# The retention blocks of a hybrid decoder layer: three products as f32 matmuls without splits, a mean of squares on ACT, a third raw weight buffer

## The chip, the cores and the metric

One core of one Trainium2 chip runs the whole kernel in one launch. The metric is the device time of an execution in microseconds (us), lower is better. The engines are TensorE (PE; its weight loads are shown as PEld), VectorE (DVE), ScalarE (ACT), GpSimd (POOL) and SyncE (SP), which only issues DMAs here.

## The reference

One inference step of a one-layer decoder, with a prompt of 1,024 positions and 8 samples of 4 positions, model width 1,024, all in f32. One input projection gives the columns of sliding-window attention, of retention (4 heads, key width 128, value width 256), of the retention gate and of two merge gates. The change is in the retention branch, which goes through the prompt in chunks of 128 positions:

```
scores = einsum('bihd,bjhd->bhij', q, k) * dmask
inner  = einsum('bhij,bjhe->bihe', scores, v)
cross  = einsum('bihd,bhde->bihe', q, s0) * q_decay
s_new  = exp(log_g * L) * s0 + einsum('bjhd,bjhe->bhde', k * k_decay, v)
o      = inner + cross
o      = o * rsqrt(mean(o * o, axis=-1) + EPS)      # per head, then silu(gate) * o
```

After it come two output projections, the merge through `w_o`, and a convolutional feed-forward of width 3 x 1,024.

## The kernel before, in words

**Products.** Most matmuls are done on split operands: a value x is written as hi = x rounded to fp32r (a copy on ACT) and lo = x - hi (on DVE or POOL; helper `split`, lines L228 and L223, on POOL L225), and `mm3` makes a product as hi·hi + hi·lo + lo·hi, three fp32r matmuls (L255, L256, L257). Operands that are plain f32 go to TensorE unsplit in a few places, the scores (L1113) and the sample attention (L731) among them.

**The stream.** The projections of the 16 pairs of column blocks (queries and keys, gates, merge gates) are a Python generator `stream`. Each pair has two halves j of the columns (528 of the 1,056 each), each half seven products of a Strassen-like scheme (A11, S1, A22, S2, A12, S4, S3), each product twelve matmuls of 264 columns into banks `ps_q`. ACT copies results out (L898); DVE adds others (L921 for S4, L923 for S3). `adv(n)` makes the generator go on by n products, so that other work can be traced between them.

**Weights of the stream.** `in_split(n)` loads the two raw weight tiles of a pair (`pair_weights`, L340 on the SP queue, 512 KB each) and makes seven split operands of them, one for each product (`w_split`: ACT L329, DVE L223). The buffer of every third raw tile comes from `wx["raw"]`, the others from the pool `wraw` of two; before the change `wx["raw"]` is `wraw` too, so there are two raw buffers in all. The operands of a pair are made while the second half of the pair before runs; its raw loads are traced at A22 in the first half of that pair.

**The sample blocks** come first between the products: `sample(h)` for 4 heads, each with 4 steps over pairs of samples. A step takes a state tile `s0` of 256 KB (loaded by `load_s0` on SP, L989; shown in the profile as `s`), splits it, makes its products with `kb` (L1033, L1035), updates it (L1036) and stores it from the POOL queue (L1038); three stream products stand between steps. `finish` is the per-head norm.

**The prompt blocks**: 32 blocks g, 8 for each head, are pipelined by hand. `front(g)` makes scores and the transpose of k (L1113, L1114) into one bank `ps_a` of two, masks the scores (L1116) and makes the split operands `sT`, `kt`, `vt`, `qs`; it is traced one block ahead, and `load_qk` (SP, L1084, three buffers) and `load_v` (POOL, L1091, four buffers) two blocks ahead of it. `middle(g)` makes inner and cross product into one bank and the state's product into another, updates `state` (L1144), splits it into `sts` for the next block, and calls `finish`. `tail(g)` of the block before turns the result by TensorE (L979) and multiplies it with the gate (L1163). Four stream products are traced with each block. In some blocks the tail also makes sums of `w_r` and `w_down` weights (`zt`) and stores.

**finish** squares with a sum along the row on ACT (L971), makes mean and epsilon on DVE (`rsqrt_mean`, L280), the power -0.5 on POOL (L282), and scales on ACT (L973).

**What sets the order.** The Tile framework turns the traced program into one instruction list for each engine: a scheduler places instructions by priority in traced order and by its own simulated times, and gives a pool's buffer to the next tile once all readers of the old one are placed. On the chip each engine and each DMA queue (SP's and POOL's) then works strictly through its list.

Of the kernel before, what the change touches and what calls it, by code (L numbers as in the profile page):

```python
# [9 lines left out]
F32 = mybir.dt.float32  # L10
# [3 lines left out]
ALU = mybir.AluOpType  # L14
# [106 lines left out]
def trunk(ctx, tc, I, O):  # L121
# [95 lines left out]
    def f32(ap):  # L217
        return ap.bitcast(F32)
# [546 lines left out]
    pa = ppool("pa", 2, ps_stack)  # L765
    pq = ppool("pq", 1, ps_stack)
    pb = ppool("pb", 2, ps_stack)
    wx["sum"], wx["raw"] = pool("wsum", 1, stack=sm_stack), wraw
    p2 = pool("p2", 1, stack=ph_stack)

    def quarters(t):
# [36 lines left out]
    def ST(name, shape, dt=F32, **kw):  # L808
        return rp.tile(list(shape), dt, name=name, **kw)
# [64 lines left out]
    def stream():  # L874

        early = (A11, S1, S2, A12, S4, S3)
        ws = in_split(ORDER[0])
        next(ws)
        ops = {p: next(ws) for p in early}
        last, nh = None, 0  # L880
        for i, n in enumerate(ORDER):
            for j in range(2):
                o = TT("pair")
                c11, c12, c21, c22 = (o[:, HW * q:HW * q + HW] for q in range(4))
                dst = {A12: c11, S1: c22, S2: c12, A22: c21}
                bk = [psum(pq, "q%d" % b)[:, :HW] for b in (0, 2)]
                b1 = pq.tile([P, 512], F32, name="ps_q1", tag="q1", bufs=2)[:, :HW]
                bk.insert(1, b1)
                if j:
                    nxt = {}  # L890

                def product(p, ps, t, j, dst):
                    for k in range(4):
                        xh, xl = xop(ex1, p, j, k)
                        mm3(ps, t[:, k], t[:, 4 + k], xh, xl, p in (A11, S1) and k == 0, k == 3,
                            skip_group_check=p not in (A11, S1))
                    if p in dst:
                        S.copy(out=dst[p], in_=ps)  # L898

                for p in (A11, S1, A22, S2, A12, S4, S3):  # L900
                    if p == A22:
                        if last is not None:
                            product(A22, *last)
                        if j == 0:
                            ops[A22] = next(ws)
                            if i + 1 < len(ORDER):
                                ws = in_split(ORDER[i + 1])
                                next(ws)
                        if last is not None:
                            yield  # L910
                        continue
                    if p == S2:
                        if nh < 2:
                            TE.matmul(bk[1], ops[p][:, 0], xop(ex1, p, j, 0)[0], start=True, stop=True)
                            S.copy(out=bk[1], in_=bk[0])
                        nh += 1
                    product(p, bk[{A11: 0, A12: 0, S2: 1, S3: 1, S1: 2, S4: 2}[p]], ops[p], j, dst)
                    if p == A11 and nh >= 2:
                        S.copy(out=bk[1], in_=bk[0])
                    if p == S4:  # L920
                        V.tensor_tensor(out=c12, in0=bk[2], in1=c12, op=add)  # L921
                    if p == S3:
                        V.tensor_tensor(out=c22, in0=bk[1], in1=c22, op=add)  # L923
                    if p == S2:
                        flush()
                    if j and i + 1 < len(ORDER):
                        nxt[p] = next(ws)
                    yield
                last = bk[1], ops[A22], j, dst
                PEND.append((pairs[n][2], j, o))  # L930
            if i + 1 < len(ORDER):
                ops = nxt
        product(A22, *last)
        flush()
        yield
# [31 lines left out]
    def finish(po, n, s, h, bufs=2):  # L967

        ssq = sml.tile([P, 1], F32, name="ss")[:n]
        o = ST("o", (P, 256), bufs=bufs)[:n]  # L970
        S.activation(o, po[:n, :256], AF.Square, accum_out=ssq)  # L971
        r = rsqrt_mean(ssq, 256, n, 1, oeps[:n, s, h:h + 1])
        S.mul(o, po[:n, :256], r)  # L973
        return o

# [8 lines left out]
    def load_s0(n):  # L984
        if n >= 2 * DB:
            return
        h, bb = n // 4, 2 * (n % 4)
        s0s_[n] = ST("s0", (P, 2, 256), bufs=4)
        ld.dma_start(out=s0s_[n], in_=I["state_ret"][0, bb:bb + 2, h].rearrange("b k e -> k b e"))  # L989

    def sample(h):
        gS = float(GAMMA[h] ** 4)
        dm = ST("dm", (P, P), bufs=2)
        ld.dma_start(out=dm, in_=I["dmask"][:, h, 1])
        qk8 = ST("qk8", (P, 2, NS), bufs=2)
        ld.dma_start(out=qk8, in_=qk_d[h].rearrange("i p t -> p i t")[:, :, :NS])
# [2 lines left out]
        r8 = ST("r8", (P, 2, P))  # L999
        for i in range(2):  # L1000
            S.copy(out=r8[:, i, :].rearrange("p (o t) -> p o t", o=4), in_=rep(qk8[:, i]))
        v8 = ST("v8", (P, 256), F32R, bufs=2)
        S.copy(out=v8[0:32], in_=vs)
        S.copy(out=v8[64:96], in_=vs)
        V.tensor_tensor(out=v8[32:64], in0=vs, in1=f32(v8)[0:32], op=sub)
# [14 lines left out]
        TE.matmul(po, h8[:, 0, 0:2 * NS], v8, start=True, stop=False)  # L1020
        for bb in range(0, DB, 2):
            s0 = s0s_[(h * DB + bb) // 2]
            load_s0((h * DB + bb) // 2 + 2)
            s0s = ST("s0s", (P, 2, 2, 256), F32R)
            split(s0s[:, 0], s0s[:, 1], s0)
            for b in range(2):
                q = q8[:, 2 * NS * (bb + b):2 * NS * (bb + b + 1)]
                for s in range(2):
                    TE.matmul(po, q, s0s[:, s, b], start=False, stop=bb + b == DB - 1 and s == 1)
            pk = ps_a()  # L1030
            for b in range(2):
                kb = ST("kb", (P, P), F32R, bufs=2)
                V.tensor_scalar(out=kb, in0=f32(h8)[:, 1], scalar1=bm[:, bb + b:bb + b + 1],  # L1033
                                scalar2=None, op0=mult)
                TE.matmul(pk[:, 256 * b:256 * b + 256], kb, v8, start=True, stop=True)  # L1035
            V.scalar_tensor_tensor(out=s0, in0=s0, scalar=gS,  # L1036
                                   in1=pk.rearrange("p (b e) -> p b e", b=2), op0=mult, op1=add)
            st.dma_start(out=O["ret_sample"][0, bb:bb + 2, h].rearrange("b k e -> k b e"), in_=s0)  # L1038
            yield
# [2 lines left out]
        V.tensor_tensor(out=os8, in0=po[0:NS], in1=os8, op=add)  # L1042
        S.copy(out=z8[:, h], in_=turn(pt, finish(os8, NS, 1, h, 1)))

    for n in range(2):
        load_s0(n)
    adv(18)
    for h in range(4):
        for _ in sample(h):
# [36 lines left out]
    def load_v(g):  # L1086
        if g >= NBLK:
            return
        h, tt = divmod(g, NB)
        vts[g] = ST("vt", (P, 2, 256), F32R, bufs=4)  # L1090
        st.dma_start(out=f32(vts[g][:, 1]), in_=v_d[h, tt])  # L1091

    def mask(h):
        dm = ST("dm", (P, P), bufs=2)
# [13 lines left out]
    def front(g, dm):  # L1108
        h, tt = divmod(g, NB)
        q, k = (qks[g][:, i] for i in range(2))  # L1110
        vt = vts[g]
        ps = ps_a()
        TE.matmul(ps[:, :P], k, q, start=True, stop=True)  # L1113
        TE.transpose(ps[:, P:2 * P], k, ident)  # L1114
        s32 = ST("s32", (P, P))
        V.tensor_tensor(out=s32, in0=ps[:, :P], in1=dm, op=mult)  # L1116
        sT = ST("sT", (P, 2, P), F32R, bufs=2)
        split(sT[:, 0], sT[:, 1], s32)
        kt = ST("kt", (P, 2, P), F32R, bufs=2)
        S.mul(kt[:, 0], ps[:, P:2 * P], kdec[:, 0, h:h + 1])  # L1120
        V.scalar_tensor_tensor(out=kt[:, 1], in0=ps[:, P:2 * P], scalar=kdec[:, 0, h:h + 1],
                               in1=f32(kt)[:, 0], op0=mult, op1=sub)
        split(vt[:, 0], vt[:, 1], f32(vt[:, 1]))
        qs = None
        if tt:
            qs = ST("qs", (P, 2, P), F32R, bufs=2)
            split(qs[:, 0], qs[:, 1], q, G)
        return ps, sT, kt, vt, qs

    def middle(g, ps, sT, kt, vt, qs):  # L1130
        h, tt = divmod(g, NB)
        gL = float(GAMMA[h] ** 128)
        vh, vl = vt[:, 0], vt[:, 1]
        pt = ps_b()
        po = pt[:, :256]
        mm3(po, sT[:, 0], sT[:, 1], vh, vl, True, tt == 0)
        if tt:
            sts = state["sts"]
            mm3(po, qs[:, 0], qs[:, 1], sts[:, 0], sts[:, 1], False, True)
        pk = ps[:, 256:]  # L1140
        mm3(pk, kt[:, 0], kt[:, 1], vh, vl, True, True)
        ns_ = ST("state", (P, 256), bufs=2)
        if tt:
            V.scalar_tensor_tensor(out=ns_, in0=state["s"], scalar=gL, in1=pk, op0=mult, op1=add)  # L1144
        else:
            V.tensor_copy(out=ns_, in_=pk)
        state["s"] = ns_
        if tt < NB - 1:
            sts = state["sts"] = ST("sts", (P, 2, 256), F32R)
            split(sts[:, 0], sts[:, 1], ns_)  # L1150
        else:
            st.dma_start(out=O["ret_prompt"][0, 0, h], in_=ns_)
        return pt, finish(po, P, 0, h)

# [566 lines left out]
```

## Time and profile before

| | |
|---|---|
| median of 3 runs | 1690.79 us (1689.51 to 1692.35) |
| the profiled execution's own time | 1689.79 us |
| its span, first to last instruction | 1688.0 us |
| mean granted TensorE clock | 0.992 |
| instructions | 32,984 |
| DMA | 273.92 MB, mean 162 GB/s |
| stream of the 16 pairs, by the starts of its matmuls | 273 to 729 us of the span |
| sample blocks, by the starts of their state products | 335 to 444 us |
| prompt blocks, by the starts of their scores and products | 456 to 698 us |

Busy times are shares of the span of one profiled execution. The records of matmuls are pipelined: a matmul of 264 columns is recorded with some 284 ns, and the next starts some 120 ns later, so prices of matmuls are taken from start to start. A wait on the weight load (PEld) and one on the matmul that follows it are the same stand of TensorE seen twice.

### The profile page before, as it was taken

What the parts mean: (1) busy time and instruction counts of PE and PEld (TensorE: products, weight loads), DVE (VectorE), ACT (ScalarE), POOL (GpSimd) and SP (SyncE); (2) the same over time, 40 slices, a digit from 0 to 9 for tenths busy, and PEclk for the clock granted to TensorE, in tenths of its full rate; (3) what the DMA queues carried; (4) which work ended last, traced back from release to release, by engine and by line L of the source; (5) the groups of instructions that cost most, each with busy time, mean ns of one, the idle gap of its engine ahead of it and who ended that gap; (6) DMA issues with size and microseconds to landing.
All of it is one profiled execution on the core that took longest, in us unless ns stands there. A gap on an engine that the chain in (4) does not pass through costs nothing.

```text
span 1688.0 us, 32984 instructions
## 1 busy us (share of the span) xinstructions
PE 1633.9 (97%) x12643; PEld 1591.9 (94%) x12643; DVE 1273.3 (75%) x2227; ACT 870.0 (52%) x1942; POOL 499.1 (30%) x714
## 2 busy tenths in 40 slices
PE   8999999888989999999899999999999999999997
PEld 7999989888989989999778999999999999999997
DVE  7887737799677777658857888888888888445476
ACT  6566534444656665564433555555555556444343
POOL 4232420356344443341312122212313323111101
PEclk9999999999999999999999999999999999999999
DMA  7212222435777677596721244454444447866655
GB/s 198 66 45 73 82 63 103 147 124 168 225 230 230 202 246 222 194 296 205 229 94 68 64 141 159 150 161 148 152 146 146 146 146 254 256 184 201 196 175 157
DMA packets 273295, 273.92 MB, mean 162 GB/s; under 512 B 23040, under 2 KB 234272, under 8 KB 273121
## 3 DMA queue, kind: packets, MB, share of 16 engines
q1 hardware_dynamic: 239377, 155.25, 31.7%
q0 software_dynamic: 33760, 116.57, 19.9%
q8 instruction: 99, 1.62, 0.4%
q14 instruction: 59, 0.48, 0.1%
HBM read 184.24 MB, written 87.49 MB: 161 GB/s over the span
## 4 chain that ended last, share of the span: by engine, by line
PE 74%; DVE 9%; DMA 8%; issue 3%; ACT 3%; POOL 1%; SPq 0%; DVEq 0%; ACTq 0%; POOLq 0%
PE ps_m L256 9%; PE ps_m L257 9%; PE ps_m L255 9%; PE ps_t L256 7%; PE ps_t L255 7%; PE ps_t L257 7%; PE ps_q L255 3%; PE ps_q L257 3%; PE ps_q L256 3%; PE ps_mm L255 3%; PE ps_mm L256 3%; PE ps_mm L257 3%; DMA w_raw<-in_w_in 2%; DVE w L223 1%; DMA w_raw<-in_w_r_proj 1%
## 5 line engine op out<-in xcount | busy, mean ns | idle before, releaser
L255 PE MATMUL ps_q<-xh,w 128*128 128x264 f32 x512 | 150.6, 294 | 10.0 <-DVE pair L921 6.4
L223 DVE SCALAR_TENSOR_TENSOR w_lo<-w_raw,w_hi 128x1024 fp32r<-128x1024 f32 x83 | 104.8, 1268 | 65.8 <-ACT w_hi L228 61.3
L255 PE MATMUL ps_t<-xh,w_hi 128*128 128x264 f32 (+2 forms) x524 | 148.9, 284 | 0.0
L256 PE MATMUL ps_t<-xl,w_hi 128*128 128x264 f32 (+2 forms) x524 | 148.7, 284 | 0.0
L257 PE MATMUL ps_t<-xh,w_lo 128*128 128x264 f32 (+2 forms) x524 | 148.0, 283 | 0.0
L256 PE MATMUL ps_q<-xl,w 128*128 128x264 f32 x512 | 147.0, 287 | 0.0
L257 PE MATMUL ps_m<-xh,w_lo 128*128 128x264 f32 x512 | 145.5, 284 | 1.5 <-DVE w_lo L223 1.5
L257 PE MATMUL ps_q<-xh,w 128*128 128x264 f32 x512 | 146.3, 287 | 0.0
L255 PE MATMUL ps_m<-xh,w_hi 128*128 128x264 f32 x512 | 145.9, 285 | 0.0
L256 PE MATMUL ps_m<-xl,w_hi 128*128 128x264 f32 x512 | 145.5, 284 | 0.0
L223 DVE SCALAR_TENSOR_TENSOR w<-w_raw,w 128x512 fp32r<-128x512 f32 x152 | 110.3, 730 | 26.4 <-ACT w L329 25.3
L1471 DVE SCALAR_TENSOR_TENSOR c_out<-u_ext,fconst,c_out 128x1024 f32<-128x1024 f32 x96 | 122.0, 1281 | 2.6 <-ACT c_out L1467 0.5
L228 ACT CAST w_hi<-w_raw 128x1024 fp32r<-128x1024 f32 x62 | 65.2, 1051 | 107.0 <-PE ps_t L256 74.5
L255 PEld LDWEIGHTS ps_q<-xh,w 128*128 128x128 f32 x512 | 97.8, 191 | 12.9 <-DVE pair L921 8.4
L329 ACT CAST w<-w_raw 128x512 fp32r<-128x512 f32 x152 | 94.1, 621 | 27.0 <-DVE w_raw L223 15.1
L257 PEld LDWEIGHTS ps_t<-xh,w_lo 128*128 128x128 f32 x524 | 98.8, 188 | 0.0
L256 PEld LDWEIGHTS ps_t<-xl,w_hi 128*128 128x128 f32 x524 | 98.6, 188 | 0.0
L255 PEld LDWEIGHTS ps_t<-xh,w_hi 128*128 128x128 f32 x524 | 98.6, 188 | 0.0
L257 PEld LDWEIGHTS ps_m<-xh,w_lo 128*128 128x128 f32 x512 | 96.3, 188 | 1.9 <-DVE w_lo L223 1.9
L256 PEld LDWEIGHTS ps_q<-xl,w 128*128 128x128 f32 x512 | 97.9, 191 | 0.0
L257 PEld LDWEIGHTS ps_q<-xh,w 128*128 128x128 f32 x512 | 97.6, 191 | 0.0
L223 DVE SCALAR_TENSOR_TENSOR xl<-t,xh 128x1056 fp32r<-128x1056 f32 (+1 forms) x53 | 67.7, 1280 | 39.0 <-ACT xh L228 38.9
(468 smaller groups left out, 6233.2 us busy)
## 6 DMA issues: line engine op xcount, KB each, us to landing
w_raw<-in_w_up SPq DMA_DIRECT2D x48, 512.0 KB, 4.1
w_raw<-in_w_in SPq DMA_DIRECT2D x42, 512.0 KB, 4.6
w_raw<-s_d SPq DMA_DIRECT2D x60, 256.0 KB, 3.7
t_d<-t POOLq DMA_DIRECT2D x24, 528.0 KB, 4.1
t<-t_d POOLq DMA_DIRECT2D x24, 528.0 KB, 5.0
t<-in_w_down SPq DMA_DIRECT2D x40, 256.0 KB, 4.6
s_d<-t POOLq DMA_DIRECT2D x20, 512.0 KB, 3.7
w_raw<-in_w_down SPq DMA_DIRECT2D x36, 256.0 KB, 4.9
```

Of the source, the lines that this page charges most:

```text
L223: pinned(V.scalar_tensor_tensor(out=out, in0=in0, scalar=1.0, in1=in1, op0=mult, op1=op))
L228: pinned(S.copy(out=hi, in_=src))
L255: TE.matmul(ps, wh, xh, start=start, stop=False, **kw)
L256: TE.matmul(ps, wh, xl, start=False, stop=False, **kw)
L257: TE.matmul(ps, wl, xh, start=False, stop=stop, **kw)
L329: S.copy(out=t[:, 0:4], in_=src)
L1471: V.scalar_tensor_tensor(out=c[:, NS:], in0=u[:, g, NU + t:NU + t + SEQ], scalar=sc[t], in1=c[:, NS:], op0=mult, op1=add)
```

## The change

The prompt blocks keep `sT`, `kt`, `vt`, the queries and the state as plain f32 and make each of the three products with one f32 matmul. `finish`, which prompt and sample blocks share, scales inside the square (1/16 squared is 1/256) and adds epsilon with an ACT instruction. The pool `wsum`, of one buffer for each tag, also holds every third raw weight tile, and the pair after next is asked for at S4 in the second half of a pair. Some sample tiles get fewer buffers: the state tile 3 instead of 4, loaded one step ahead instead of two; `dm` and `v8` one instead of two.

```diff
-    wx["sum"], wx["raw"] = pool("wsum", 1, stack=sm_stack), wraw
+    wx["sum"] = wx["raw"] = pool("wsum", 1, stack=sm_stack)
...
         ops = {p: next(ws) for p in early}
+        coming = in_split(ORDER[1])
+        next(coming)
...
                             ops[A22] = next(ws)
-                            if i + 1 < len(ORDER):
-                                ws = in_split(ORDER[i + 1])
-                                next(ws)
+                            ws = coming
...
                         nxt[p] = next(ws)
+                        if p == S4 and i + 2 < len(ORDER):
+                            coming = in_split(ORDER[i + 2])
+                            next(coming)
...
-        S.activation(o, po[:n, :256], AF.Square, accum_out=ssq)
-        r = rsqrt_mean(ssq, 256, n, 1, oeps[:n, s, h:h + 1])
+        S.activation(o, po[:n, :256], AF.Square, scale=1 / 16, accum_out=ssq)
+        ms = sml.tile([P, 16], F32, name="ms")[:n, :1]
+        S.activation(ms, ssq, AF.Identity, bias=oeps[:n, s, h:h + 1])
+        r = sml.tile([P, 16], F32, name="rs")[:n, :1]
+        G.tensor_tensor(out=r, in0=ms, in1=mhalf[:n, :1], op=ALU.pow)
...
-        s0s_[n] = ST("s0", (P, 2, 256), bufs=4)
+        s0s_[n] = ST("s0", (P, 2, 256), bufs=3)
...
-        dm = ST("dm", (P, P), bufs=2)
+        dm = ST("dm", (P, P))
...
-        v8 = ST("v8", (P, 256), F32R, bufs=2)
+        v8 = ST("v8", (P, 256), F32R)
...
-            load_s0((h * DB + bb) // 2 + 2)
+            load_s0((h * DB + bb) // 2 + 1)
...
-        vts[g] = ST("vt", (P, 2, 256), F32R, bufs=4)
-        st.dma_start(out=f32(vts[g][:, 1]), in_=v_d[h, tt])
+        vts[g] = ST("vt", (P, 256), bufs=4)
+        st.dma_start(out=vts[g], in_=v_d[h, tt])
...
-        s32 = ST("s32", (P, P))
-        V.tensor_tensor(out=s32, in0=ps[:, :P], in1=dm, op=mult)
-        sT = ST("sT", (P, 2, P), F32R, bufs=2)
-        split(sT[:, 0], sT[:, 1], s32)
-        kt = ST("kt", (P, 2, P), F32R, bufs=2)
-        S.mul(kt[:, 0], ps[:, P:2 * P], kdec[:, 0, h:h + 1])
-        V.scalar_tensor_tensor(out=kt[:, 1], in0=ps[:, P:2 * P], scalar=kdec[:, 0, h:h + 1],
-                               in1=f32(kt)[:, 0], op0=mult, op1=sub)
-        split(vt[:, 0], vt[:, 1], f32(vt[:, 1]))
-        qs = None
-        if tt:
-            qs = ST("qs", (P, 2, P), F32R, bufs=2)
-            split(qs[:, 0], qs[:, 1], q, G)
-        return ps, sT, kt, vt, qs
+        sT = ST("sT", (P, P), bufs=2)
+        V.tensor_tensor(out=sT, in0=ps[:, :P], in1=dm, op=mult)
+        kt = ST("kt", (P, P), bufs=2)
+        S.mul(kt, ps[:, P:2 * P], kdec[:, 0, h:h + 1])
+        return ps, sT, kt, vt, q
...
-        mm3(po, sT[:, 0], sT[:, 1], vh, vl, True, tt == 0)
+        TE.matmul(po, sT, vt, start=True, stop=tt == 0)
         if tt:
-            sts = state["sts"]
-            mm3(po, qs[:, 0], qs[:, 1], sts[:, 0], sts[:, 1], False, True)
+            TE.matmul(po, q, state["s"], start=False, stop=True)
         pk = ps[:, 256:]
-        mm3(pk, kt[:, 0], kt[:, 1], vh, vl, True, True)
+        TE.matmul(pk, kt, vt, start=True, stop=True)
...
-        if tt < NB - 1:
-            sts = state["sts"] = ST("sts", (P, 2, 256), F32R)
-            split(sts[:, 0], sts[:, 1], ns_)
-        else:
+        if tt == NB - 1:
             st.dma_start(out=O["ret_prompt"][0, 0, h], in_=ns_)
```

More of the change, by code (lines that the diff above doesn't have):

```diff
@@ L1043, in sample @@
         S.copy(out=z8[:, h], in_=turn(pt, finish(os8, NS, 1, h, 1)))
-    for n in range(2):
-        load_s0(n)
+    load_s0(0)
     adv(18)
@@ L1114, in front, with middle @@
         TE.transpose(ps[:, P:2 * P], k, ident)
-        s32 = ST("s32", (P, P))
-        V.tensor_tensor(out=s32, in0=ps[:, :P], in1=dm, op=mult)
-        sT = ST("sT", (P, 2, P), F32R, bufs=2)
-        split(sT[:, 0], sT[:, 1], s32)
-        kt = ST("kt", (P, 2, P), F32R, bufs=2)
-        S.mul(kt[:, 0], ps[:, P:2 * P], kdec[:, 0, h:h + 1])
-        V.scalar_tensor_tensor(out=kt[:, 1], in0=ps[:, P:2 * P], scalar=kdec[:, 0, h:h + 1],
-                               in1=f32(kt)[:, 0], op0=mult, op1=sub)
-        split(vt[:, 0], vt[:, 1], f32(vt[:, 1]))
-        qs = None
-        if tt:
-            qs = ST("qs", (P, 2, P), F32R, bufs=2)
-            split(qs[:, 0], qs[:, 1], q, G)
-        return ps, sT, kt, vt, qs
-    def middle(g, ps, sT, kt, vt, qs):
+        sT = ST("sT", (P, P), bufs=2)
[3 more added lines that the diff above has]
+        return ps, sT, kt, vt, q
+    def middle(g, ps, sT, kt, vt, q):
         h, tt = divmod(g, NB)
         gL = float(GAMMA[h] ** 128)
-        vh, vl = vt[:, 0], vt[:, 1]
         pt = ps_b()
         po = pt[:, :256]
-        mm3(po, sT[:, 0], sT[:, 1], vh, vl, True, tt == 0)
+        TE.matmul(po, sT, vt, start=True, stop=tt == 0)
         if tt:
-            sts = state["sts"]
-            mm3(po, qs[:, 0], qs[:, 1], sts[:, 0], sts[:, 1], False, True)
+            TE.matmul(po, q, state["s"], start=False, stop=True)
         pk = ps[:, 256:]
-        mm3(pk, kt[:, 0], kt[:, 1], vh, vl, True, True)
+        TE.matmul(pk, kt, vt, start=True, stop=True)
         ns_ = ST("state", (P, 256), bufs=2)
```

## The prediction

> **What bounds the kernel now.** I read the page first, for the busy shares, then the busy time by stage, then the waits inside the stage that the change touches, then single tiles and lines for prices.
>
> ```profile
> PE 1633.9 (97%) x12643; PEld 1591.9 (94%) x12643; DVE 1273.3 (75%) x2227; ACT 870.0 (52%) x1942; POOL 499.1 (30%) x714
> ```
> ```profile
> 270.00:450.00 180.00, 165.78 (x1251) 160.73 (x1250) 148.21 (x247) 79.89 (x186) 77.43 (x74) 0.98 0.44 146
> 450.00:700.00 250.00, 237.89 (x1909) 232.96 (x1908) 183.57 (x474) 147.44 (x415) 107.43 (x174) 0.99 0.72 224
> ```
> ```profile
> 450.00:500.00 50.00, 45.10 (x343) 0.93 0.81 253
> ```
>
> The first fence is the page's line of busy times; the others are busy times by stretch (start:end, length, then PE, PEld, DVE, ACT, POOL, the granted clock, the DMA share and GB/s; the last row was asked for PE alone). TensorE is busy 97% of the span, so a gain must come from its idle time or its work. The sample blocks lie in 270 to 450 us, the 32 prompt blocks in 450 to 700, both woven into the stream of 16 input-projection pairs. Outside them the change does nothing. TensorE's idle time is 14.2 us in the first stretch (180 - 165.78) and 12.1 in the second (250 - 237.89). A low clock adds some: 0.93 over 50 us is 3.5 us of work lost in the second stretch, 0.98 over 180 us is 3.6 in the first. So the pool that the prompt stage can give back is 12.1 + 3.5 = 15.6 us, the sample stage's 17.8. DVE is the busiest of the others in both (82% and 73%).
>
> What ends the waits in 450 to 700 us (waiter, whom it waited for: us in total, times, longest us):
>
> ```profile
> PEld ps_a L1113 <- DVE state L1144: 5.3, 5, 2.3
> PEld ps_q L255 <- DVE pair L921: 4.8, 6, 1.9
> PEld ps_b L979 <- ACT o L973: 2.6, 4, 1.1
> PEld ps_q L255 <- ACT pair L898: 1.6, 1, 1.6
> ```
> ```profile
> DVE vt L223 <- ACT vt L228: 13.9, 10, 4.0
> DVE s L223 <- DMA w_raw<-in_w_in: 10.4, 7, 2.9
> ```
> ```profile
> POOL rs L282 <- DVE ms L280: 17.5, 13, 3.5
> ACT vt L228 <- DMA vt<-v_d: 23.2, 12, 6.5
> ```
>
> TensorE stands mostly for DVE: for the state update that frees a score bank, and for the pair addition that frees a projection bank. DVE in turn stands in its queue for the split of V, which stands in ACT's queue for V's load, and for a raw weight load. Those two stalls are what the change takes out of the queues.
>
> **The change part by part.** Prices of what goes (tile queries: minimum/median/maximum ns):
>
> ```profile
> L228 ACT CAST sT<-s x32: 285/299/307, 459.0 to 687.6; 128x128 fp32r<-128x128 f32 x32
> L223 DVE SCALAR_TENSOR_TENSOR sT<-s,sT x32: 281/286/722, 459.5 to 688.3; 128x128 fp32r<-128x128 f32 x32
> ```
> ```profile
> L228 ACT CAST vt<-vt x32: 394/407/426, 456.4 to 673.5; 128x256 fp32r<-128x256 f32 x32
> L223 DVE SCALAR_TENSOR_TENSOR vt<-vt x32: 414/422/672, 456.9 to 674.7; 128x256 fp32r<-128x256 f32 x32
> ```
> ```profile
> L228 ACT CAST qs<-qk x28: 284/296/322, 454.3 to 684.2; 128x128 fp32r<-128x128 f32 x28
> L225 POOL TENSOR_TENSOR qs<-qk,qs x28: 447/475/1354, 454.7 to 684.6; 128x128 fp32r<-128x128 f32 x28
> ```
> ```profile
> L228 ACT CAST sts<-state x28: 402/406/418, 462.8 to 691.6; 128x256 fp32r<-128x256 f32 x28
> L223 DVE SCALAR_TENSOR_TENSOR sts<-state,sts x28: 409/420/736, 463.7 to 692.0; 128x256 fp32r<-128x256 f32 x28
> ```
> ```profile
> L1121 DVE SCALAR_TENSOR_TENSOR kt<-ps_a,kdec,kt x32: 340/347/353, 459.7 to 688.5; 128x128 fp32r<-128x128 f32 x32
> ```
> ```profile
> L280 DVE TENSOR_SCALAR ms<-ss,oeps x36: 195/208/217, 360.6 to 699.0; 128x1 f32<-128x1 f32 x32, 32x1 f32<-32x1 f32 x4
> ```
>
> 1. Splits gone. DVE loses 32 x (0.286 + 0.422 + 0.347 + 0.208 for the mean) + 28 x 0.420 = 52.2 us, so 183.6 becomes about 131 of 250 us. ACT loses 32 x (0.299 + 0.407) + 28 x (0.296 + 0.406) = 42.3 us, POOL 28 x 0.475 = 13.3. None of it is TensorE time; it counts only through shorter queues. The state's way to the next cross product loses 0.41 + 0.42 us and two hops.
>
> 2. Products. Each block had three groups of three fp32r matmuls, now three f32 matmuls (two in the four first blocks): 28 x 3 + 4 x 2 = 92 products. Both prices are in the timeline (start us, us, engine, line, operation):
>
> ```profile
> 186.26 1.02 PE L731 MATMUL ps_a<-ckT,qs 128*128 128x512 f32 x2
> 186.72 0.68 PE L255 MATMUL ps_mm<-w_hi,xh 128*128 128x256 f32 x1
> 187.24 0.28 PE L256 MATMUL ps_mm<-w_lo,xh 128*128 128x256 f32 x1
> ```
> ```profile
> 563.67 0.28 PE L255 MATMUL ps_b<-vt,sT 128*128 128x256 f32 x1
> ...
> 564.74 0.28 PE L255 MATMUL ps_q<-xh,w 128*128 128x264 f32 x1
> ```
>
> From the second fence, nine fp32r matmuls take 1.07 us from start to start: 0.119 each, 0.357 a group. The page calls both kinds f32; L731's operands alone are plain f32, and one such matmul is issued as two passes (x2). From 186.26 to 187.24 lie one f32 product of 512 columns and one fp32r matmul: 0.98 - 0.12 = 0.86 us, so 0.43 for 256 columns. Each product costs 0.073 us more: 92 x 0.073 = **+6.7 us**, on the busiest engine, with nothing to hide it.
>
> This row meets a rule of the Trainium skill, FP8 and Floating Point Precision, section TensorE Precision Notes: a true FP32 product is four passes through the array. Four passes at the 0.119 of an fp32r matmul would be 0.476 us, and the step +10.9 instead of +6.7; the row shows 0.43, so the measurement decides, and the dearer figure weighs only toward the slower side.
>
> 3. Queues of the prompt stage. Of the 15.6 us pool, the four TensorE rows above tell which share hangs on whom: 10.1 of 14.3 us is DVE, 4.2 ACT. DVE's two quoted blocks (13.9 + 10.4 us) go, one with the V split, one with the earlier raw load; DVE's load falls by 28% and ACT's by 23 to 24%. Bounds: nothing (the waits move to the next late thing, zt and gate loads) to all 15.6. I take two thirds, **-10.4**, because both blocks at the head of the DVE queue vanish and what is late next is shorter.
>
> 4. Mean on ACT. An added ACTIVATE of one column, 36 times. Its price lies between the read of an accumulator and a biased ACTIVATE of 32 columns:
>
> ```profile
> L971 ACT ACTIVATION_READ_ACCUMULATOR o<-ps_b x32: 190/200/227, 461.6 to 698.5; 128x1 f32 x32
> ```
> ```profile
> L1466 ACT ACTIVATE c_out<-u_ext,fconst x48: 407/425/467, 939.0 to 1419.1; 128x32 f32<-128x32 f32 x48
> ```
>
> I take 0.25, near the one of equal width: +8 us of ACT in 32 blocks (6.4 to 13.6), under a load that falls by 42.3, so nothing on the path. It spares POOL its 17.5 us behind DVE (L282), and behind POOL stand L973 and the transposes L979 (the 2.6 us above, inside the pool). The Trainium skill (ScalarE: Activation LUTs, What ACT_TABLE_LOAD costs) puts an ACTIVATE with a pointer bias at about 280 ns plus 0.83 per element; by it the 32 would be 9 us, still hidden.
>
> 5. Third raw buffer. The two loads of pair i+1 were traced at A22 in the first half of pair i, and are now at S4 in the second half of pair i-1, four products earlier. The second tile waits on SP until step S3 has used the older one; behind it stand query/key, gate and weight-sum loads. Gain in the prompt stage: counted in 3. In the sample stage DVE keeps its kb, rope and split work (148 of 180 us), so of its 17.8 us pool I take **-2**, bounds 0 and -6.
>
> 6. Smaller sample buffers. A state tile is loaded one step ahead instead of two, into a buffer that must first be stored:
>
> ```profile
> 380.30 0.53 SPq L989 DMA_DIRECT2D s<-in_state_ret  x1
> 385.35 0.65 SPq L989 DMA_DIRECT2D s<-in_state_ret  x1
> ```
> ```profile
> 383.31 0.62 ACT L228 CAST s0s<-s 128x512 fp32r<-128x512 f32 x1 [1.09 <-DVE sh L822]
> 389.04 0.61 ACT L228 CAST s0s<-s 128x512 fp32r<-128x512 f32 x1
> ```
> ```profile
> DMA to landing us min/median/max: 2.6/2.7/5.3
> ```
>
> The two loads are issued where a store frees a buffer. With three buffers they would carry the tiles that ACT splits at 383.31 and 389.04: landing at 380.30 + 2.7 = 383.0 and 388.05, spare 0.3 and 1.0 us. The same reckoning leaves under 2 us for three more of the 13 reloads, five in all. Bounds 0 to 5 x (5.3 - 2.7) = +13 us of ACT waiting; I take **+0.5**, since at the median landing all are in time and ACT is 44% busy there. The single buffers of dm and v8 cost nothing: their last readers are some steps back.
>
> 7. The key/query tile now stays until the cross product, over half a block later, so its load (L1084, three buffers) starts later. Before block 31 the cross product of block 28 starts at 675.2 and the scores at 686.6: 11.4 us, against
>
> ```profile
> DMA to landing us min/median/max: 2.1/4.2/7.4
> ```
>
> so it is hidden: 0, at most 4 us if the SP queue holds it up.
>
> **Sum** against the profiled execution (1689.8 us, of which 1688.0 span; the median of the runs is 1690.8): +6.7 - 10.4 - 2 + 0.5 = -5.2, so 1684.6, and with the median 1.0 higher I say **1685**.
>
> **The rivals.**
> - *TensorE stays the bound and the stalls only change their name* (slower). The +6.7 is certain; if less than 6.7 us of the pools comes back, the change loses. For it: 95% busy in the stage, DMA at 0.72, other loads queued behind the same waits. Against it: DVE ends 10.1 of 14.3 us, and its load falls most. With 1 to 3 us back: 1694 to 1696.
> - *A wash*: 4 to 9 us back against 6.7, 1687.5 to 1694. The raw loads may gain nothing, since the second tile of a pair is still freed late: then the 10.4 us of DVE waits stay, and with them about 4 us of the pool.
> - *Nearly the whole pool*: 15.6 + 4 - 6.7 = -13, 1677. For it: a granted clock of 0.93 recovers only if gaps disappear. Against: ACT pair copies and the sample stage's DVE stay.
> - *Late state tiles* (part 6): if three of five land 2 us late and TensorE stands, +6, which decides from about 5 us on: 1691 to 1697.
>
> **How the numbers follow.** 0.2% is 3.4 us, about what a measurement of this kernel tells from no change. Chances: forecast (1680 to 1687) 0.45; nearly the whole pool 0.15; wash 0.2; TensorE bound 0.14; late tiles 0.06. So faster 0.60, same 0.20, slower 0.20. The likeliest one's own range is 1680 to 1687; the range from nearly the whole pool to TensorE bound with the dearer product is 1675 to 1697.
>
> **What would show it.** Right: in 450 to 700 us DVE falls to about 131 and ACT to about 113 us; the waits on vt, sts and rs behind DVE are gone; L255 to L257 no longer carry ps_b; a product of 256 columns shows two passes 0.21 us apart; raw weight loads land well ahead of the first split; the granted clock in 450 to 500 rises. Wrong: TensorE idles as long as before, now behind key/query loads, V loads or zt; ACT waits for state tiles at the sample splits; or the f32 product costs other than 0.43 us.

## The result and the profile after

The changed kernel takes 1697.31 us (median of 6, 1693.39 to 1699.95) against 1689.39 for the kernel before (6 runs, 1686.78 to 1692.35): ratio 1.0044, 95% interval 1.0030 to 1.0058. It is 7.9 us slower, where 5 us faster was forecast. The profiled execution has a span of 1695.1 us against 1688.0. Every trace below is of a single execution; those of e1 (1699.99 us) and e15 (1700.12) are the longest of their kernels, and one execution of e15 of 3233.4 us is in neither its ratio nor its time.

In the code of after, lines have moved by up to 12: L1118 and L1119 are the scores and the transpose of k, L1121 `sT`, L1123 `kt`, L1131, L1133 and L1135 the three products, L1138 the state, L1154 the gated output z, L1089 `load_qk`, L1096 `load_v`, L1105 the gate load, L900 the pair copy, L974, L976 and L979 square, mean and scale, L985 the transposes. L340 and L223 are as before.

The page's busy times, then the busy times by stretch (columns as in the prediction), for after; the row in the last fence is before's, for 500 to 550 us:

```profile
PE 1637.6 (97%) x12551; PEld 1593.2 (94%) x12551; DVE 1227.7 (72%) x2067; ACT 852.1 (50%) x1858; POOL 485.2 (29%) x686
```
```profile
270.00:450.00 180.00, 162.78 (x1242) 157.43 (x1242) 146.47 (x241) 80.27 (x187) 75.72 (x68) 1.00 0.42 140
450.00:700.00 250.00, 237.49 (x1767) 230.68 (x1766) 141.39 (x313) 126.85 (x324) 89.43 (x149) 0.97 0.72 226
```
```profile
450.00:500.00 50.00, 44.58 (x315) 42.95 (x314) 24.20 (x56) 22.86 (x60) 15.03 (x26) 0.93 0.63 202
500.00:550.00 50.00, 44.90 (x324) 43.43 (x323) 24.51 (x55) 26.36 (x64) 19.01 (x33) 0.93 0.69 222
550.00:600.00 50.00, 50.00 (x385) 48.88 (x384) 30.69 (x68) 27.60 (x69) 20.55 (x34) 1.00 0.79 241
```
```profile
500.00:550.00 50.00, 47.64 (x394) 47.22 (x393) 36.44 (x94) 31.21 (x84) 20.38 (x34) 1.00 0.70 224
```

DVE fell from 183.6 to 141.4 us of work in the prompt stage, ACT and POOL fell too, and TensorE still idles 12.5 us (250 - 237.49; before 12.1). And the clock is now 0.93 in two slices, where before had it in one: 7 us of lost work instead of 3.5. The pool that was to shrink by 10.4 us grew from 15.6 to 19.5. The sample stage's pool went from 17.8 to 17.2. So +6.7 for the products, +3.9 and -0.6 make +10.0; the stream's last product ends at 737.3 us instead of 728.6, +8.7, and later stages give some of it back. The sum is a little high, because some of the low clock falls into idle time (TensorE did nothing from 505 to 507 us, at 0.72 and 0.50) and is counted twice.

The waits of TensorE's weight loads in 450 to 700 us of after (waiter, whom it waited for: us in total, times, longest):

```profile
PEld ps_a L1118 <- issue: 5.4, 2, 2.9
PEld ps_q L255 <- ACT pair L900: 5.3, 1, 5.3
PEld ps_b L1131 <- issue: 1.6, 1, 1.6
PEld ps_a L1118 <- DVE state L1138: 1.4, 3, 0.6
PEld ps_b L985 <- ACT o L979: 0.6, 1, 0.6
```
```profile
PE ps_a L1118 <- DMA qk<-qk_d: 5.0, 2, 2.7
```

A stand is a time in which TensorE does nothing because it waits. Beside before's list: the stands behind DVE's state (5.3), behind DVE's pair addition (4.8) and behind ACT's o (2.6) nearly went, as forecast. In their place stand two scores that waited for the load of their own queries and keys ("issue" at the weight load, named by the matmul's own row in the second fence), and one pair copy. Same sum, other names. The first such stand is the first scores of the stage, at 463.63 us (before: 456.0). The sync engine's queue tells why, first before's, then after's (start us, us, engine, line, operation), then after's waits in it:

```profile
434.63 0.53 SPq L1100 DMA_DIRECT2D z<-gr_d  x1
435.22 2.86 SPq L1084 DMA_DIRECT2D qk<-qk_d  x3
452.30 0.37 SPq L340 DMA_DIRECT2D w_raw<-in_w_in  x1
```
```profile
443.42 0.37 SPq L1105 DMA_DIRECT2D z<-gr_d  x1
454.42 0.37 SPq L340 DMA_DIRECT2D w_raw<-in_w_in  x1
454.88 3.59 SPq L1089 DMA_DIRECT2D qk<-qk_d  x3
```
```profile
SPq L340 <- DVE w L223: 10.6, 1, 10.6
SPq L995 <- DMA out_ret_sample<-s: 5.3, 1, 5.3
```

Before, the three loads of queries and keys were issued ahead of a raw weight load, which then waited for its buffer and held up nobody who was needed soon. After, the raw load is listed first, waits 10.6 us for DVE's last split of the older tile, and the loads behind it go out 20 us later than before. Only about half of the 20 us is this wait: the gate load ahead of it already goes out 8.8 us later than before (443.42 against 434.63), and in that stretch a sample state tile (L995) waits 5.3 us until a store has freed its buffer. In this execution the stand that follows costs twice, on TensorE's timeline and then in its clock (start:end, length, PE busy, granted clock, DMA share, GB/s):

```profile
463.63 0.46 PE L1118 MATMUL ps_a<-qk 128*128 128x128 f32 x2 [2.32 <-DMA qk<-qk_d]
```
```profile
464.00:465.00 1.00, 1.00 (x9) 0.74 1.03 400
465.00:466.00 1.00, 1.00 (x6) 0.50 1.08 380
466.00:467.00 1.00, 1.00 (x7) 0.50 0.92 282
467.00:468.00 1.00, 1.00 (x7) 0.55 0.58 173
468.00:469.00 1.00, 1.00 (x10) 1.00 0.17 50
```

2.32 us idle, and then some 3.4 us at half clock, 1.7 us of work lost. The clock is at half around the other two stands as well. It does not follow from every such stand: in e10, a run of the next section that only adds products to after, TensorE idles 2.36 us at the same place and the clock stays at 1.00:

```profile
463.40 0.46 PE L1118 MATMUL ps_a<-qk 128*128 128x128 f32 x2 [2.36 <-DMA qk<-qk_d]
```
```profile
464.00:468.00 4.00, 4.00 (x34) 1.00 0.88 297
```

The other two stands of after, and what was waited for ahead of the third:

```profile
495.46 0.77 PE L1118 MATMUL ps_a<-qk 128*128 128x128 f32 x2 [2.69 <-DMA qk<-qk_d]
507.46 0.59 PE L255 MATMUL ps_q<-xh,w 128*128 128x264 f32 x1 [4.91 <-ACT pair L900]
```
```profile
499.07 0.80 POOL L299 DMA_DIRECT2D s_d<-zt  x1 [5.56 <-DVE z L1154]
```
```profile
505.07 0.78 DVE L223 SCALAR_TENSOR_TENSOR zt<-z 128x264 f32<-128x264 f32 x2 [3.36 <-DMA s_d<-zt]
507.03 0.94 ACT L900 COPY pair<-ps_q 128x264 f32<-128x264 f32 x3 [4.07 <-DVE zt L223]
```

The third reads backwards: TensorE waits for ACT's copy, ACT for DVE's `zt`, DVE for a store that frees the `zt` buffer, and POOL could issue that store only after DVE's z of a block. Why this z came late is not shown. DVE itself had stood 5.04 us, to 496.28, for a weight-sum load; and the second stand alone is not enough, since e10 has one of 3.26 us at 492.94 and no third.

### The profile page after: what moved, and what is told of

It reads as the page before. It is cut to its first block, busy times and chain, and to the rows that moved or that the text cites. A ratio compares the mean times of both kernels' runs of the same rounds, so it can differ in the third digit from the quotient of the medians.

```text
span 1695.1 us, 32482 instructions
## 1 busy us (share of the span) xinstructions
PE 1637.6 (97%) x12551; PEld 1593.2 (94%) x12551; DVE 1227.7 (72%) x2067; ACT 852.1 (50%) x1858; POOL 485.2 (29%) x686
## 4 chain that ended last, share of the span: by engine, by line
PE 62%; DMA 5%; DVE 4%; issue 3%; ACT 1%; POOL 1%; SPq 0%; DVEq 0%; POOLq 0%; ACTq 0%
PE ps_m L257 9%; PE ps_m L255 9%; PE ps_m L256 9%; PE ps_t L256 8%; PE ps_t L255 7%; PE ps_t L257 7%; PE ps_q L255 3%; PE ps_q L257 3%; PE ps_q L256 3%; DMA zt<-in_w_down 1%; DMA a_in<-a_d 1%; PE ps_b L1131 1%; DMA qk<-qk_d 1%; PE ps_a L1135 0%; PE ps_t L459 0%
## 5 line engine op out<-in xcount | busy, mean ns | idle before, releaser
L223 DVE SCALAR_TENSOR_TENSOR w_lo<-w_raw,w_hi 128x1024 fp32r<-128x1024 f32 x83 | 104.4, 1264 | 61.8 <-ACT w_hi L228 57.6
L223 DVE SCALAR_TENSOR_TENSOR w<-w_raw,w 128x512 fp32r<-128x512 f32 x152 | 106.7, 707 | 36.1 <-ACT w L329 33.6
L255 PEld LDWEIGHTS ps_m<-xh,w_hi 128*128 128x128 f32 x512 | 96.3, 188 | 0.2
```

What stands on the lines that cost most here:

```text
L223: pinned(V.scalar_tensor_tensor(out=out, in0=in0, scalar=1.0, in1=in1, op0=mult, op1=op))
L255: TE.matmul(ps, wh, xh, start=start, stop=False, **kw)
```

## The experiments

All ratios are to the kernel before, run on the same chip, with 95% intervals. 0.2% is 3.4 us.

**The change in parts.** The products alone, the products with the mean on ACT, the sample buffers alone, and the whole change with a fourth query and key buffer. The third raw buffer was not tried alone.

```diff
# e1_products: before, with only the hunks of load_v, front, middle (f32 products)
# e4_prod_mean: e1 and the hunk of finish (mean on ACT)
# e5_sample: before, with only bufs of s0, dm, v8 and load_s0 one step ahead
# e6_after_qk4: after, and
-        qks[g] = ST("qk", (P, 2, P), bufs=3)
+        qks[g] = ST("qk", (P, 2, P), bufs=4)
```

> The kernel before with the f32 products of the prompt blocks alone (no splits of sT, kt, vt, queries, state); the mean, the raw buffers and the sample buffers stay. Theory P (the products lose by themselves: 92 x 0.073 = +6.7 us of TensorE, and the DVE stalls that go are replaced by late key/query loads, whose buffer is now held until the cross product): +4 to +8 us, ratio 1.0025 to 1.005. Theory R (the third raw buffer and the smaller sample buffers lose, the products gain): -2 to -6 us, ratio 0.9965 to 0.999.

Measured: 1.0020 (1.0006 to 1.0034), 1691.35 us, a little under theory P's range and far from the gain of R. The products alone cost less than their 6.7 us (0.0020 is 3.4 us), so their shorter queues seem to give something back, but not enough.

> The kernel before with the f32 products and the mean on ACT, but two raw buffers and the old sample buffers: the change without its third part. Both theories put the mean at within 1.5 us of e1_products, since ACT has room. P: ratio 1.002 to 1.005, as with the whole change. R: 0.996 to 0.999.

Measured: 1.0049 (1.0037 to 1.0061), 1698.62 us: with the mean added, all of the loss of the whole change is there, without a third raw buffer and without the sample part. Both theories had it within 1.5 us of e1; it is 4.9 us above (0.0029).

> The kernel before with the smaller sample buffers alone (state tile 3 instead of 4 and one step ahead, dm and v8 single). If these cost what the prediction gave to late state tiles as a rival: +3 to +8 us, with ACT or TensorE waiting for state loads between 334 and 450 us. P: within 2 us of before.

Measured: 0.9994 (0.9982 to 1.0006), 1688.13 us. Alone, the smaller sample buffers cost nothing that shows; the rival of late state tiles falls.

> The changed kernel with four instead of three buffers for the key/query tile of the prompt blocks. If the late key/query loads are what the change lost by (their 5.0 us of TensorE waits in two places and the low clock behind them): 4 to 7 us under the changed kernel, ratio to before 1.000 to 1.002, and no wait of the scores on the load. If the SP queue is what holds those loads (raw weight loads standing ahead of them), a fourth buffer changes nothing: 1.004.

Measured: 1.0016 (1.0006 to 1.0027), 1692.52 us, 4.7 us under after (0.0028 of 1689). The second stand behind a key load is gone; the first is still there, at 2.6 us:

```profile
PE ps_a L1118 <- DMA qk<-qk_d: 2.6, 1, 2.6
```

**Is the mean the culprit?** The mean alone on ACT, and after with its mean back on DVE, with three and with four query and key buffers.

```diff
# e7_mean: before, with only the hunk of finish
# e8_after_dve: after without the hunk of finish
# e9_after_dve_qk4: e8 with the four buffers of e6
```

> The kernel before with the mean of squares on ACT alone. Theory M (the mean on ACT loses: ACT is in order, and what stands behind the mean, the power on POOL and the scaling, now stands behind ACT's own queue and holds the pair copies): +3 to +7 us, ratio 1.002 to 1.004, as e4_prod_mean stood 6 to 7 us above e1_products. Theory O (that difference comes only from the new order of the instruction lists together with the products): within 2 us of before.

Measured: 1.0043 (1.0028 to 1.0058), 1695.89 us: 36 short instructions on an engine that is half idle cost 7 us.

> The changed kernel with the mean back on DVE and POOL: f32 products, third raw buffer, smaller sample buffers. M: 3 to 7 us under the changed kernel, ratio to before 1.000 to 1.0025. O: 1.003 to 1.006.

Measured: 1.0052 (1.0033 to 1.0071), 1697.6 us.

> The changed kernel with the mean back on DVE and POOL and four key/query buffers. If the mean (M) and the key/query buffer (4.7 us by e6_after_qk4) add up: ratio to before 0.996 to 0.999, faster than both kernels. O: 1.001 to 1.003, no better than e6_after_qk4.

Measured: 1.0038 (1.0023 to 1.0053), 1695.65 us.

So it is not a price of the mean: added to before it costs 7 us, taken out of after it returns nothing, and the four buffers that gave 4.7 us with the mean on ACT give 2 with it on DVE, inside the intervals; e9 is slower than both forecasts. The parts do not add. What e7 shares with after is the order of the sync engine's list, though its weight buffers are those of before; e4, e8 and e9 have the raw load ahead of these loads too:

```profile
451.04 0.37 SPq L340 DMA_DIRECT2D w_raw<-in_w_in  x1
451.50 4.65 SPq L1087 DMA_DIRECT2D qk<-qk_d  x3
```
```profile
PE ps_a L1116 <- DMA qk<-qk_d: 2.4, 1, 2.4
```

**Is TensorE's time paid in full?** After, with the state's product issued twice into the same bank (the result is that of the second).

```diff
+        TE.matmul(pk, kt, vt, start=True, stop=True)
         TE.matmul(pk, kt, vt, start=True, stop=True)
```

> The changed kernel with the state's f32 product issued twice in each of the 32 blocks, into the same bank, so that the second replaces the first: one suspected cost added, 32 x 0.432 = 13.8 us of TensorE. Theory P (TensorE time in this stage counts in full): +11 to +15 us over the changed kernel, ratio to before 1.011 to 1.013. If the stage has slack from waits of other engines (the stalls would absorb it): +4 to +9, ratio 1.007 to 1.010.

Measured: 1.0124 (1.0107 to 1.0141), 1709.93 us. 32 products of 0.432 us are 13.8 us; it came to 0.0080 of 1689, 13.5 us over after. Nothing in this stage of after hides the added products.

**The order of the loads.** Theory H: what the change loses beyond the products is the raw load that waits ahead of the first query and key loads. Two edits set the order: loads held in the order in which the program asks for them (`pin`, which the kernel has), and the raw tiles of one or two pairs asked for half a pair later, as before did.

```diff
         ins = ld.dma_start(out=qks[g], ...)
+        if g < 3:
+            pin(ins)
...
             ins = ld.dma_start(out=raw, ...)
+            if 13 <= NRAW[0] <= 20:     # 18 in e11, e15 and e16
+                pin(ins)
...
-                        if p == S4 and i + 2 < len(ORDER):
+                        if p == S4 and i + 2 < len(ORDER) and i not in (4, 5):   # e12, e13
...
                         if j == 0:
                             ops[A22] = next(ws)
+                            if i - 1 in (4, 5):
+                                coming = in_split(ORDER[i + 1])
+                                next(coming)
                             ws = coming
# e11: e7 with the pins. e12: after with all of this. e13: e12 with four query and key buffers.
# e14: e1 with four query and key buffers, no pins.
```

> Before with the mean of squares on ACT alone (whose time was 1.0043 of before), and the first three loads of query and key put ahead of the raw weight load that stood before them in the list of the sync engine. Theory H (the raw load, which waits for its buffer at the head of that list, holds back the loads behind it): the first three query and key loads are issued near 435 us instead of 451.5, the stand of 2.7 us at the first scores and the lowered clock after it go, and the time falls by 3 to 7 us, to 0.9995 to 1.0025 of before. Theory P (the mean's own small instructions on ACT and POOL lengthen the chain of a block): nothing changes, 1.004. Theory L (a list in another order shifts waits about, and this one is only the most visible): the stand at the first scores goes, others take its place, and the time stays between 1.003 and 1.005.

Measured: 1.0023 (1.0012 to 1.0035), 1692.79 us. The three loads went out at 436.29 us, no score waited for one, and 3.4 us of the 7.3 came back (0.0020 of 1689), which lies in the range of H and under that of L. The rest did not come back: other waits, for DVE's z and pair, took their place, as theory L has it.

> The changed kernel with the first three query and key loads put ahead of the raw loads of the pairs at places 6 and 7 of the order, which are asked for half a pair later, as in the kernel before. Theory H: the loads are issued near 436 us instead of 454.9, the first scores start near 456 instead of 463.6, the end of the stream comes 3 to 6 us earlier, 1.0005 to 1.0025 of before. Theory T (TensorE's own +6.7 us is the whole of it): no change from 1.0044.

Measured: 0.9993 (0.9984 to 1.0002), 1687.92 us: 8.6 us under after (0.0051 of 1689), beyond what H forecast, though the loads did not get near its 436 us. The queue, the stage and the waits of e12 (its line numbers are 5 to 7 higher than those of after):

```profile
448.97 3.72 SPq L1094 DMA_DIRECT2D qk<-qk_d  x3
```
```profile
450.00:700.00 250.00, 242.12 (x1829) 234.14 (x1828) 144.44 (x320) 131.23 (x333) 90.76 (x151) 0.99 0.72 227
```
```profile
450.00:500.00 50.00, 45.59 (x331) 43.06 (x330) 27.40 (x63) 25.73 (x67) 19.57 (x33) 0.98 0.80 248
500.00:550.00 50.00, 49.25 (x376) 47.61 (x376) 27.08 (x59) 27.24 (x64) 18.14 (x31) 0.98 0.71 225
```
```profile
PEld ps_a L1125 <- DVE state L1145: 5.7, 5, 3.5
PEld ps_b L1138 <- issue: 1.6, 1, 1.6
PEld ps_b L990 <- ACT o L984: 1.6, 2, 1.0
PEld ps_a L1125 <- DVE sT L1128: 1.2, 1, 1.2
```

The loads leave only 6 us earlier than in after, because the queue still waits ahead of them, 9.1 us of it for the store that frees a state tile's buffer. But the first scores, now at 459.2 us, no longer stand for them, nor do any later ones, and the third stand is gone too. The stand behind DVE's state is back at 5.7 us. TensorE idles 7.9 us instead of 12.5, the clock is back at 0.98 where it was 0.93, and the stream ends at 728.6, where it ended before.

> The same with four query and key buffers, which takes away the second stand (2.97 us near 495 us) as well. Theory H and the buffer together: 0.998 to 1.001 of before, the best of the f32 kernels. Theory T: as the changed kernel with four buffers, 1.0016.

Measured: 1.0018 (1.0004 to 1.0032), 1690.77 us. That is outside the range of H and at the 1.0016 of theory T. The fourth buffer adds nothing once the order is right, and may cost; its one profiled execution, the shortest of the twelve (span 1684.7 us), is as short as that of e12, and what sets the others apart is open.

> Before with the three f32 products alone and four query and key buffers: no mean on ACT, no third raw buffer. The products alone took 1.002. If the query and key buffer, held until the cross product, is what the products cost beside their 6.7 us, 0.999 to 1.001; if the f32 products' own TensorE time counts in full and nothing comes back for it, 1.002 to 1.004.

Measured: 0.9993 (0.9983 to 1.0003), 1688.05 us, 4.6 us under the products alone. There the loads had been held up by another wait: in e1 they went out at 446.23 us, after 11.7 us behind the store of a sample state, and the second scores stood 2.8 us; here the first of them went at 436.92, with no such stand.

**The order, or the pins?** A control holds loads without bringing the query and key loads ahead; its pair differs from it in one raw request; and before and the products alone are treated alike.

```diff
# e15_after_pins: after with the pins only (two raw loads stay ahead)
# e16_after_qkfirst2: e15, and the raw request deferred for i = 5 alone
# e17_before_pins, e18_products_pins: before and e1 with the pins (13 to 20)
```

> The changed kernel with its raw loads 13 to 18 and its first three query and key loads held to the order in which the program asks for them, which leaves two raw loads ahead of the query and key loads in the sync engine's list. A control for the runs with these loads put ahead. Theory H (the raw load at the head of the list is the cause): the first query and key loads are issued at 450 us or later, the stand at the first scores stays, 1.003 to 1.006 of before. Theory F (holding the loads to an order is itself what brought the changed kernel back to 0.9993): 0.999 to 1.0015.

Measured: 1.0037 (1.0023 to 1.0051), 1694.38 us.

> The same, but the raw load of the pair at place 7 of the order asked for half a pair later, so that the list is that of the control up to these loads and then has the first three query and key loads ahead of the raw loads. Theory H: 0.9985 to 1.0015 of before, 4 to 9 us under the control. Theory F: as the control.

Measured: 1.0007 (0.9996 to 1.0018), 1690.53 us: 5.1 us under its control (0.0030 of 1689). The two queues, e15's and then e16's:

```profile
444.32 12.31 SPq L340 DMA_DIRECT2D w_raw<-in_w_in  x2
456.72 3.77 SPq L1091 DMA_DIRECT2D qk<-qk_d  x3
```
```profile
449.51 4.46 SPq L1094 DMA_DIRECT2D qk<-qk_d  x3
```

And whom the scores waited for, e15's and then e16's:

```profile
PE ps_a L1122 <- DMA qk<-qk_d: 2.8, 2, 2.3
```
```profile
PE ps_a L1125 <- DMA qk<-qk_d: 0.2, 1, 0.2
```

> Before with raw loads 13 to 20 and the first three query and key loads held to the program's order; its query and key loads stood ahead already. Theory H: no change, 0.998 to 1.001. Theory F: 0.993 to 0.997, so that the f32 products still lose against a before treated alike.

Measured: 1.0018 (1.0007 to 1.0029), 1691.59 us, outside both forecasts.

> Before with the f32 products alone (1.002) and the same holding of the loads. Theory H: no change from 1.002, since its query and key loads stood ahead of the raw load already. Theory F: 0.997 to 1.000.

Measured: 1.0016 (1.0004 to 1.0028), 1691.54 us. Theory F falls: the pins by themselves help neither after (e15) nor before (e17) nor the products (e18). Beside each other, e17 and e18 say what the products are worth when these loads are held in both: 1.0018 and 1.0016, nothing either way. Their lists are still not the same: in e18 the key loads go out at 444.04 us, in e17 at 434.53, and a score of e18 stands 3.05 us for its load. In the same way e11 (1.0023) beside e17 (1.0018) leaves less than 1 us for the mean, inside the intervals.

H holds for the changed kernel: twice an edit made for the order brought back 5 to 9 us, and its control without the order, e15, next to nothing (1.0037 for 1.0044). All runs beside e10, which adds work, fit: with the raw load ahead, after, e4, e7, e8, e9 and e15 lie at 1.0037 to 1.0052 and e6, with its fourth buffer, at 1.0016; with the first key loads ahead, e1, e5, e11 to e14 and e16 to e18 lie at 0.9993 to 1.0023. Two things stay open. The edit also asks for one or two pairs of raw tiles later, and no run moved the key loads with the raw requests left where they are. And the order is not the whole of what moves these kernels: e11 has the right order and stays at 1.0023, and e17 lost 0.18% by two held groups of loads. Each edit reorders the lists of all engines, and differences of up to 4 us between lists (e11, e13, e17) are left here without a named cause.

## Why the prediction was wrong, point by point

**The step that failed is part 3**, "I take two thirds, **-10.4**, because both blocks at the head of the DVE queue vanish and what is late next is shorter." The pool grew by 3.9 us instead. Its first half was right in part: TensorE's waits on DVE and on ACT's o went from after's list, nearly by size, but of the two blocks only the V split vanished; DVE's wait for raw weights grew (part 5). The second half was a guess about what is late next, and the thing late next was not shorter: key loads stuck in a queue, 5.4 us at the scores, and a pair copy, 5.3 us. With the key loads in time, in e12, TensorE stands 5.7 us behind DVE's state again, as before (5.3). In e12, with the order mended, the pool is 7.9 us idle and 2.0 of clock (0.98 in two slices of 50 us), 9.9 instead of 15.6: part 3 is then worth -5.7, not -10.4, and with +6.7 that is +1.0, near the no-change that e12 measures (0.9993).

- **Part 1** (splits gone): the direction was right, with DVE at 141 and ACT at 127 us in the stage instead of 131 and 113. The windows do not hold quite the same work, since the stage started later; but the whole execution falls short too, DVE by 45.6 us (1273.3 - 1227.7) for 52.2 and ACT by 17.9 for 42.3 less the mean's 10.6. One reason can be read in after's timeline: neighbouring records overlap (DVE's z at 489.17 is recorded with 0.42 us, and the next instruction starts at 489.50), so a sum of recorded times overstates busy time. Whether that is all of it is not shown.
- **Part 2** (products, +6.7): right. Two passes a product, and 0.43 us from one product to the next, in after's timeline:

```profile
499.80 0.60 PE L1131 MATMUL ps_b<-vt,sT 128*128 128x256 f32 x2
500.23 0.59 PE L1133 MATMUL ps_b<-state,qk 128*128 128x256 f32 x2
500.66 0.59 PE L1135 MATMUL ps_a<-vt,kt 128*128 128x256 f32 x2
501.10 0.59 PE L1131 MATMUL ps_b<-vt,sT 128*128 128x256 f32 x2
```

  e10 shows that added products count in full. The Trainium skill (FP8 and Floating Point Precision, TensorE Precision Notes) has four passes; at 0.119 us each they would be 0.476, and this trace does not agree: 0.43.
- **Part 4** (mean on ACT, nothing on the path): the instruction was priced well, 0.295 us against 0.25, and ACT had the room:

```profile
L976 ACT ACTIVATE ms<-ss,oeps x36: 289/295/312, 356.7 to 706.6; 128x1 f32<-128x1 f32 x32, 32x1 f32<-32x1 f32 x4
```

  The Trainium skill (ScalarE: Activation LUTs, What ACT_TABLE_LOAD costs) puts an ACTIVATE with a pointer bias at about 280 ns plus 0.83 per element, and this row agrees. Yet in e7 the edit cost 7 us. Of these e11, with the order set, brought 3.4 back, and beside e17, whose loads are held too, less than 1 us is left. A price hidden on its engine said nothing about the list that the edit makes.
- **Part 5** (third raw buffer, "gain in the prompt stage: counted in 3"): DVE's waits for raw weights did not go. They rose from 10.4 to 23.4 us:

```profile
DVE s L223 <- DMA w_raw<-in_w_in: 23.4, 8, 4.2
```

  The prediction named the mechanism, "The second tile waits on SP until step S3 has used the older one; behind it stand query/key, gate and weight-sum loads", and then gave it no price. As far as the runs on the order show, that wait at the head of the queue was the price and not DVE's own: e12 loses nothing, and its DVE still waits 20.5 us for raw weights. The sample stage gave 0.6 us of the 1.5 counted in parts 5 and 6.
- **Part 6** (late state tiles, +0.5): about right for ACT; e5 shows nothing. What it left out is the queue: in after the late state tile stands 5.3 us ahead of the key loads.
- **Part 7** ("hidden: 0, at most 4 us if the SP queue holds it up"): the bound was near the value. The second stand was 2.69 us, and a fourth buffer took it away and gave 4.7 us (e6). The queue may have had its part, since a weight-sum load stood at its head for 5.1 us, to 489.80; the two are not separated. The 11.4 us of cover were taken from one block late in the stage.
- **The sum**: the median's 1.0 was to be added to 1684.6, which is 1685.6 and not 1685; this decides nothing.
- **The rivals**: what came is nearest to the first, "the stalls only change their name", forecast at 1694 to 1696 with a chance of 0.14; 1697.3 lies 1.3 us above it because the pool grew instead of shrinking by 1 to 3 us.

## What to carry to other kernels

When an edit lets a load be asked for earlier than its buffer comes free, price what stands behind it in the same issuing queue: here edits that put the needed loads ahead of a 10.6 us wait brought back 5 to 9 us, as much as the dearer products cost (6.7). Taking work off a busy helper engine gives back less than its waits show (5.7 of 15.6 us here, with the order right), while products added to the engine that is 95% busy counted in full (e10). And where a scheduler makes the lists, read the order of the loads in the new list first: an edit that costs nothing on its engine can move them, so an ablation measures the list as much as the part.

## What the runs showed of the hardware that was not expected

A stand of 2.32 us on TensorE was followed by some 3.4 us of half clock (0.50 in the rows from 465 to 467 us), so that this late load of 2.3 us cost about 4 us in all. It need not come so: after 2.36 us in e10, at the same place, and after 3.05 us in e18, at 456.75 us, the granted clock stayed at 1.00. What decides it is open. The clock gate's rule in the Trainium skill (TensorE: Matmul & The Clock Gate, HAM oscillation — how this bites in real kernels) names idle gaps above about 3.4 us; the half clock agrees with it, but in after a shorter gap was enough.

A plain f32 product of 256 columns costs 0.43 us, only a fifth more than three fp32r matmuls at 0.357, and needs no split. Whether it gains where TensorE has spare time is not shown here.
